# Fewer operations per reciprocal-root iteration, and VectorE in GpSimd's place for one group of subtractions

## The chip, the cores and the metric

The kernel runs on one core of a Trainium2 chip. The metric is the device time in microseconds (us) of one execution. The engines are called as the profile calls them: PE is TensorE (matmuls; PEld are its weight loads), DVE is VectorE, ACT is ScalarE, POOL is GpSimd, SP is SyncE, which here only issues DMAs. Each engine works through its own queue of instructions in order, and waits on semaphores for the others.

## The reference, cut to what matters

One layer of an encoder: a modulated RMSNorm of x (2048 tokens of width 1024), one wide input projection, two branches (neighbourhood attention with 8 heads, and a bidirectional mLSTM with 4 heads, run over chunks of tokens), an output projection, a residual sum and a last RMSNorm.

```python
h = rmsnorm(h_res, norm_w[l]) * (1.0 + scale[:, None, :]) + shift[:, None, :]
...
proj = h @ w_in + b_in
...
na_out = neighbourhood_attention(na_q, na_k, na_v, rpb) * jax.nn.silu(na_z)
...
hm = (h_fwd + h_bwd).transpose(0, 2, 1, 3) * jax.nn.sigmoid(ml_o).reshape(B, T, ML_HEADS, ML_HEAD_DIM)
mu = jnp.mean(hm, axis=-1, keepdims=True)
var = jnp.mean(jnp.square(hm - mu), axis=-1, keepdims=True)
hm = ((hm - mu) * lax.rsqrt(var + EPS)).reshape(B, T, ML_W) * ml_norm_w
...
return rmsnorm(h_res, final_norm_w).astype(x.dtype)
```

Reciprocal roots occur in three places: in the first RMSNorm, in the normalisation of `hm`, and in the last RMSNorm.

## The kernel before, in words

Every large product is computed in three passes over split operands: a float32 value is written as a high part (rounded to the matmul's format) and a low part (the rest), and the products high·high, high·low and low·high are summed. So each block of weights has to be split before PE can use it: ACT copies the raw weights into the high tile (`whi`), and another engine subtracts the high tile from the raw one to give the low tile (`wlo`).

The program has these stages. `start` (to about 142 us) loads x, computes the first norm's roots for four groups of four token tiles, transposes, and multiplies the first two weight blocks. `tok_blocks` and `conv_blocks` (to about 500 us) multiply further blocks and convolve. `phase1b` (to about 990 us) is the mLSTM: for each head a first pass (state updates `wv`, `dc`, `st`) and a second pass (scores `a`, weighted into `ck`; the sums `pi` and `px`, combined in `num`; the ratio `r`; the head output `hm`, its moments, its root `rstd`, its mean `mu`; then ACT normalises `hm`, and PE turns it into `ht`). The mLSTM's own matmuls are small, so PE is filled up with the rest of the input projection: `nq_gen` is a generator that yields after each of its matmuls (tile `pq`), and `pump(n)` draws n of them into the program between the mLSTM's steps. `phase2` is the attention and the output projection.

The projection inside `nq_gen` uses weight tiles of 128 columns, the *side weights*. Each is loaded by SP (`rawq`, L919) into the one buffer there is for it, split by `nq_split` into one half of `whi_a` and `wlo_a`, and used for one, two or four groups of 512 tokens. There are 30 such splits. In 20 of them (`s < 12`) the high part is a plain copy on ACT (L927) and POOL subtracts (L928). In the other 10, which hold the queries, ACT also scales (L930), and DVE makes the low part in one fused instruction (L931). The load of the next raw weights waits until the subtraction has read the buffer.

`rsqrt` (L1269) makes a reciprocal root on DVE: a first guess by integer operations on the bits (L1275, L1276), and three Newton iterations y ← y·(1.5 − 0.5·v·y²). With more than one value per partition an iteration has four instructions (L1282 to L1285); with one value the first two are fused (L1280). It is called four times in `start` (L251, four values per partition), 16 times in the mLSTM (L1210, four values) and 16 times in `phase2` (L1529, one value).

`start` and `phase2` are in an order written by hand. Between them a scheduler places each engine's instructions from the program's order and its own estimates, so a change of engine or of the number of operations there also moves neighbours.

Of the kernel before, what the change touches and what calls it, by code (L numbers as in the profile page):

```python
# [8 lines left out]
F32 = mybir.dt.float32  # L9
F32R = mybir.dt.float32r  # L10
AF = mybir.ActivationFunctionType
ALU = mybir.AluOpType
# [3 lines left out]
P = 128  # L16
# [42 lines left out]
class Kernel:  # L59
# [862 lines left out]
    def nq_split(self, i, s, raw):  # L922
        nc = self.nc
        hi, lo = self.wslot[0]
        cs = slice((i % 2) * P, (i % 2 + 1) * P)
        if s < 12:
            nc.scalar.activation(hi[:, :, cs], raw, AF.Copy)  # L927
            nc.gpsimd.tensor_tensor(lo[:, :, cs], raw, hi[:, :, cs].bitcast(F32), ALU.subtract)  # L928
        else:
            nc.scalar.activation(hi[:, :, cs], raw, AF.Copy, scale=-0.125)  # L930
            nc.vector.scalar_tensor_tensor(lo[:, :, cs], raw, -0.125, hi[:, :, cs].bitcast(F32), ALU.mult, ALU.subtract)  # L931
# [334 lines left out]
                    load_z(NG - 1)  # L1266
            yield

    def rsqrt(self, pool, y, v, nm, eng=None):  # L1269

        nc = self.nc
        eng = eng or nc.vector
        I32 = mybir.dt.int32
        n = y.shape[-1]
        nc.vector.tensor_scalar(y.bitcast(I32), v.bitcast(I32), 1, None, ALU.logical_shift_right)  # L1275
        nc.vector.tensor_scalar(y.bitcast(I32), y.bitcast(I32), -1, 0x5F3759DF, ALU.mult, ALU.add)  # L1276
        t = pool.tile([P, n], F32, tag="nwt", bufs=2, name=f"nwt_{nm}")
        for _ in range(3):
            if n == 1:
                nc.vector.scalar_tensor_tensor(t, y, v, y, ALU.mult, ALU.mult)  # L1280
            else:
                eng.tensor_tensor(t, y, y, ALU.mult)  # L1282
                eng.tensor_tensor(t, t, v, ALU.mult)
            eng.tensor_scalar(t, t, -0.5, 1.5, ALU.mult, ALU.add)
            eng.tensor_tensor(y, y, t, ALU.mult)  # L1285


    def phase2(self):
        nc = self.nc
# [427 lines left out]
```

## Time and profile before

| | |
|---|---|
| runs shown | 1376.62, 1380.95, 1381.31 us (median 1380.95) |
| profiled execution | 1379.22 us, its span 1377.2 us |
| granted PE clock, mean of the span | 0.988 |
| low parts of side weights on POOL (L928) | 20 instructions, 48.4 us |
| low parts of side weights on DVE (L931) | 10 instructions, 12.3 us |

The profile is of one execution. Its span runs from the first to the last instruction. A row of a group gives the line, the engine, the operation, written tile and read tiles, the count, then busy us and mean ns, then the idle time ahead of it with what ended it. A row of the timeline gives start and duration in us; in brackets stands how long the engine had been idle, and for whom it waited. A row of waits gives total us, times, and the longest. The granted clock is 1.00 or 0.50 at any moment, so a mean just under one means a few short slow windows.

### The profile page before, as it was taken

Reading aid. Unit: us, or ns where it says so; the run is one execution under the profiler, and the core shown is the slowest. Engines: PE = TensorE matmul, PEld = TensorE weight load, DVE = VectorE, ACT = ScalarE, POOL = GpSimd, SP = SyncE. Lnnn points to the kernel's source line nnn. Section 1 sums busy time; section 2 is a strip of 40 time slices with the busy share of each in tenths; the row PEclk is TensorE's granted clock in tenths of the full one; section 3 lists DMA queues with packets and bytes.
Section 4 is the critical chain, followed back from the end, with each engine's and each line's share of the span. In section 5 each row is a group of like instructions: output and inputs, shape, how many; then the busy total and the mean of one; then the engine's idle time right before and its main releaser. Section 6 shows DMA issues by size and latency. Waiting matters only on the chain. (4 is left out here: it accounts for less than half of the span.)

```text
span 1377.2 us, 23246 instructions
## 1 busy us (share of the span) xinstructions
PE 1303.8 (95%) x8026; PEld 1115.6 (81%) x8026; DVE 812.0 (59%) x2583; ACT 556.1 (40%) x1178; POOL 233.0 (17%) x266
## 2 busy tenths in 40 slices
PE   2999998999999999999999998999989999999996
PEld 2899998999877788888888787788766888888885
DVE  4744323111374696267768777877546777777774
ACT  5875445432231332113323233333336555555551
POOL 1000222433010110111121012121202111112111
PEclk9999999999999999999999999999989999999998
DMA  9996487766276876455757969746788897876862
GB/s 367 286 301 147 115 219 225 209 183 192 62 176 171 209 190 184 134 163 156 227 181 214 269 196 236 210 130 177 188 221 227 196 213 169 204 184 174 193 156 76
DMA packets 272010, 266.22 MB, mean 193 GB/s; under 512 B 32746, under 2 KB 234634, under 8 KB 271894
## 3 DMA queue, kind: packets, MB, share of 16 engines
q1 hardware_dynamic: 175870, 183.58, 48.8%
q0 software_dynamic: 21632, 38.40, 11.5%
q10 hardware_dynamic: 74392, 42.76, 10.8%
q8 instruction: 64, 1.05, 0.3%
q14 instruction: 52, 0.43, 0.1%
HBM read 179.14 MB, written 93.71 MB: 198 GB/s over the span
## 5 line engine op out<-in xcount | busy, mean ns | idle before, releaser
L954 PE MATMUL pq<-hhi,whi_a 128*128 128x512 f32 x512 | 212.2, 414 | 0.0
L954 PE MATMUL pq<-hlo,whi_a 128*128 128x512 f32 x512 | 212.0, 414 | 0.0
L954 PE MATMUL pq<-hhi,wlo_a 128*128 128x512 f32 x512 | 211.6, 413 | 0.0
L1435 ACT ACTIVATE pbuf<-pbuf,mn 128x480 f32<-128x480 f32 (+5 forms) x128 | 76.4, 597 | 122.3 <-DVE mn L1434 109.1
L954 PEld LDWEIGHTS pq<-hhi,whi_a 128*128 128x128 f32 x512 | 98.6, 193 | 18.4
L954 PEld LDWEIGHTS pq<-hhi,wlo_a 128*128 128x128 f32 x512 | 98.5, 192 | 18.4
L954 PEld LDWEIGHTS pq<-hlo,whi_a 128*128 128x128 f32 x512 | 98.6, 193 | 18.0
L1508 PE MATMUL y<-hhi,whi_a 128*128 128x512 f32 x256 | 84.8, 400 | 0.4 <-ACT whi_a L1481 0.4
L1508 PE MATMUL y<-hhi,wlo_a 128*128 128x512 f32 x256 | 84.4, 399 | 0.0
L1434 DVE CUSTOM_DVE_ANT_0 pbuf<-pS,tab 128x480 f32<-128x480 f32 (+5 forms) x128 | 64.9, 540 | 31.9 <-DMA tab<-d_t 15.9
L1180 ACT ACTIVATE num<-px,gtile 128x129 f32<-128x129 f32 x120 | 38.3, 365 | 98.4 <-PE px L1175 85.4
L928 POOL TENSOR_TENSOR wlo_a<-rawq,whi_a 128x1024 fp32r<-128x1024 f32 x20 | 48.4, 2421 | 163.1 <-ACT whi_a L927 122.1
L1107 DVE TENSOR_SCALAR wv<-kv,gtile 128x129 f32<-128x129 f32 x120 | 37.5, 318 | 61.4 <-PE dc L1123 33.4
L1199 POOL TENSOR_TENSOR hm<-hm,ck 128x128 f32<-128x128 f32 x64 | 26.5, 414 | 263.1 <-DVE hm L1198 220.5
L1471 PE MATMUL pO<-pt,v 128*64 128x128 f32 (+3 forms) x832 | 62.1, 283 | 8.7 <-ACT pt L1458 7.3
L803 ACT ACTIVATE dec<-dec,gtile 128x128 f32<-128x128 f32 x128 | 41.5, 391 | 66.8 <-POOL dec L799 54.4
L1471 PEld LDWEIGHTS pO<-pt,v 128*64 128x64 f32 (+3 forms) x832 | 45.8, 137 | 25.4 <-issue 12.9
L1456 PE MATMUL pT<-ident,pbuf 128*128 128x128 f32 (+2 forms) x416 | 59.9, 283 | 2.1 <-DVE pbuf L1446 2.1
L568 DVE TENSOR_TENSOR stv<-pv,brow 128x256 f32<-128x256 f32 x32 | 12.9, 423 | 78.9 <-PE pv L535 41.8
L1458 ACT ACTIVATE pt<-pT 96x384 f32<-96x384 f32 (+3 forms) x128 | 57.6, 499 | 0.7 <-PE pT L1456 0.7
L1508 PEld LDWEIGHTS y<-hhi,whi_a 128*128 128x128 f32 x256 | 47.2, 188 | 10.0 <-ACT whi_a L1481 0.6
L1456 PEld LDWEIGHTS pT<-ident,pbuf 128*128 128x128 f32 (+2 forms) x416 | 44.2, 137 | 13.4 <-issue 9.6
(301 smaller groups left out, 3556.2 us busy)
## 6 DMA issues: line engine op xcount, KB each, us to landing
ck<-d_ck SPq DMA_DIRECT2D x64, 384.5 KB
kv<-d_ck SPq DMA_DIRECT2D x120, 128.5 KB
rawq<-in_w_main_dram SPq DMA_DIRECT2D x30, 512.0 KB
raw<-in_w_main_dram SPq DMA_DIRECT2D x20, 512.0 KB
x<-in_x_dram SPq DMA_DIRECT2D x16, 512.0 KB
wmod<-in_w_mod_dram SPq DMA_DIRECT2D x16, 512.0 KB
dec<-d_mneg SPq DMA_DIRECT2D x32, 256.0 KB
d_ck<-dec ACTq DMA_DIRECT2D x32, 256.0 KB
```

The source lines that it names most:

```text
L803: nc.scalar.activation(t[:, d, o, :], t[:, d, o, :], AF.Exp, bias=self.cols["g"][:, d, h, c : c + 1])
L928: nc.gpsimd.tensor_tensor(lo[:, :, cs], raw, hi[:, :, cs].bitcast(F32), ALU.subtract)
L954: nc.tensor.matmul(patch_ps(ps) if patch else ps, w, self.htok(h, g, k, patch), start=(k == 0 and n == 0), stop=(k == KT - 1 and n == 2))
L1107: nc.vector.tensor_scalar(wv, tiles[d, i][:, 128:257], self.cols["w"][:, d, h, c : c + 1], None, ALU.mult)
L1180: nc.scalar.activation(num[:, d, :], px[:, d, :], AF.Copy, scale=self.cols["inter"][:, d, h, c : c + 1])
L1199: nc.gpsimd.tensor_tensor(t, t, vo.pop(c)[:, 129:257], ALU.mult)
L1434: nc.vector.tensor_tensor_reduce(pt[:, :nk], ps, tabs[place[u]][j][:, :nk], 1.0, 3e38, ALU.add, ALU.min, mn)
L1435: nc.scalar.activation(pt[:, :nk], pt[:, :nk], AF.Exp, bias=mn, scale=-1.0, accum_out=sums[:, j : j + 1])
L1456: nc.tensor.transpose(ps[:cs, i, :], pts[j][:, i * cs : (i + 1) * cs], self.ident)
L1458: nc.scalar.activation(t[:cs, :nch, :], ps[:cs, :nch, :], AF.Copy)
L1471: nc.tensor.matmul(po[j * HD : (j + 1) * HD, :], v[:n, h * HD : (h + 1) * HD], pt[j][:n, i, :], start=(i == 0), stop=(i == nch - 1))
L1508: nc.tensor.matmul(y, m[:, k, :], w[k][:, cs], start=(k == 4 and n == 0), stop=(k == 3 and n == 2))
```

## The change

In `nq_split` the subtraction of L928 is given to DVE; operands, shapes and result are the same. In `rsqrt` the constant −0.5 is taken out of the loop: w = −0.5·v is computed once per root into a new small tile (`nwv`), and an iteration is t = y², t = t·w, y = (t + 1.5)·y, the last two operations of that fused. A root of four values thus has 12 instructions instead of 14, and a root of one value 9 instead of 11. The argument `eng`, which no caller used, is gone. Behind `rsqrt` line numbers are one lower.

```diff
         if s < 12:
             nc.scalar.activation(hi[:, :, cs], raw, AF.Copy)
-            nc.gpsimd.tensor_tensor(lo[:, :, cs], raw, hi[:, :, cs].bitcast(F32), ALU.subtract)
+            nc.vector.tensor_tensor(lo[:, :, cs], raw, hi[:, :, cs].bitcast(F32), ALU.subtract)
...
+        w = pool.tile([P, n], F32, tag="nwv", bufs=2, name=f"nwv_{nm}")
+        nc.vector.tensor_scalar(w, v, -0.5, None, ALU.mult)
         t = pool.tile([P, n], F32, tag="nwt", bufs=2, name=f"nwt_{nm}")
         for _ in range(3):
             if n == 1:
-                nc.vector.scalar_tensor_tensor(t, y, v, y, ALU.mult, ALU.mult)
+                nc.vector.scalar_tensor_tensor(t, y, w, y, ALU.mult, ALU.mult)
             else:
-                eng.tensor_tensor(t, y, y, ALU.mult)
-                eng.tensor_tensor(t, t, v, ALU.mult)
-            eng.tensor_scalar(t, t, -0.5, 1.5, ALU.mult, ALU.add)
-            eng.tensor_tensor(y, y, t, ALU.mult)
+                nc.vector.tensor_tensor(t, y, y, ALU.mult)
+                nc.vector.tensor_tensor(t, t, w, ALU.mult)
+            nc.vector.scalar_tensor_tensor(y, t, 1.5, y, ALU.add, ALU.mult)
```

Three places show where the scheduler puts the moved subtraction; they are the places at 671, 836 and 873 us of the profile before, of which the prediction speaks. In the names the first number is the head (or the raw weight's turn), the next ones the step or chunk, the last one a running number of the tile.

DVE early in the first pass of head 1, where the last root of head 0 is finished (671 us), before:

```order
L1285 TENSOR_TENSOR rstd_0_3_6607<-rstd_0_3_6607,nwt_0_3_6611 128x4
L1133 SCALAR_TENSOR_TENSOR st_1_1_12_6690<-st_1_1_13_6666,gtile_1999,dc_1_2_6681 128x129
L1282 TENSOR_TENSOR nwt_0_3_6611<-rstd_0_3_6607 128x4
L1107 TENSOR_SCALAR wv_1_1_4_6686<-kv_1_1_11_6654,gtile_1999 128x129
L1283 TENSOR_TENSOR nwt_0_3_6611<-nwt_0_3_6611,var_0_3_6606 128x4
L1284 TENSOR_SCALAR nwt_0_3_6611<-nwt_0_3_6611 128x4
L1285 TENSOR_TENSOR rstd_0_3_6607<-rstd_0_3_6607,nwt_0_3_6611 128x4
L1212 SCALAR_TENSOR_TENSOR mu_0_3_6624<-mv_0_3_6434,rstd_0_3_6607 128x4
L1107 TENSOR_SCALAR wv_1_0_5_6713<-kv_1_0_5_6677,gtile_1999 128x129
```

The same place now:

```order
L1284 TENSOR_TENSOR nwt_0_3_6606<-nwt_0_3_6606,nwv_0_3_6604 128x4
L1133 SCALAR_TENSOR_TENSOR st_1_1_12_6682<-st_1_1_13_6658,gtile_1995,dc_1_2_6673 128x129
L1285 SCALAR_TENSOR_TENSOR rstd_0_3_6600<-nwt_0_3_6606,rstd_0_3_6600 128x4
L1107 TENSOR_SCALAR wv_1_1_4_6678<-kv_1_1_11_6646,gtile_1995 128x129
L1212 SCALAR_TENSOR_TENSOR mu_0_3_6616<-mv_0_3_6428,rstd_0_3_6600 128x4
L928 TENSOR_TENSOR wlo_a_123<-rawq_7_6498,whi_a_122 128x8x128
L1107 TENSOR_SCALAR wv_1_0_5_6705<-kv_1_0_5_6669,gtile_1995 128x129
```

The subtraction of the eighth raw weight stands on DVE behind `mu` and ahead of the `wv` of step 5; the root ends ahead of it.

DVE in the second pass of head 2 (836 us), before:

```order
L992 SCALAR_TENSOR_TENSOR qst_15_2_8565<-pq_15_2_8466,bcol_93,qst_15_2_8565 128x512
L1282 TENSOR_TENSOR nwt_2_1_8544<-rstd_2_1_8540 128x4
L1204 BN_STATS b6_2_8_8606<-hm_2_2_8531 128x6
L1283 TENSOR_TENSOR nwt_2_1_8544<-nwt_2_1_8544,var_2_1_8539 128x4
L1205 BN_AGGR mv_2_2_8532<-b6_2_8_8606 128x2
L1284 TENSOR_SCALAR nwt_2_1_8544<-nwt_2_1_8544 128x4
L1285 TENSOR_TENSOR rstd_2_1_8540<-rstd_2_1_8540,nwt_2_1_8544 128x4
L1212 SCALAR_TENSOR_TENSOR mu_2_1_8557<-mv_2_1_8326,rstd_2_1_8540 128x4
L1182 TENSOR_TENSOR num_2_9_8595<-num_2_9_8595,pi_2_9_8589 128x258
```

The same place now:

```order
L992 SCALAR_TENSOR_TENSOR qst_15_2_8551<-pq_15_2_8453,bcol_93,qst_15_2_8551 128x512
L1285 SCALAR_TENSOR_TENSOR rstd_2_1_8527<-nwt_2_1_8533,rstd_2_1_8527 128x4
L1204 BN_STATS b6_2_8_8592<-hm_2_2_8518 128x6
L1212 SCALAR_TENSOR_TENSOR mu_2_1_8543<-mv_2_1_8314,rstd_2_1_8527 128x4
L928 TENSOR_TENSOR wlo_a_123<-rawq_17_8390,whi_a_122 128x8x128
L1205 BN_AGGR mv_2_2_8519<-b6_2_8_8592 128x2
L1182 TENSOR_TENSOR num_2_9_8581<-num_2_9_8581,pi_2_9_8575 128x258
```

Here the subtraction stands behind `mu` too, but ahead of `num`, which PE's next `pi` needs.

DVE early in the first pass of head 3 (873 us), before:

```order
L1107 TENSOR_SCALAR wv_3_1_4_9010<-kv_3_1_11_8981,gtile_1999 128x129
L1282 TENSOR_TENSOR nwt_2_3_8933<-rstd_2_3_8929 128x4
L975 SCALAR_TENSOR_TENSOR hlo3_1231<-pq_9_0_8870,bcol_93,hlo3_1231 64x512
L1283 TENSOR_TENSOR nwt_2_3_8933<-nwt_2_3_8933,var_2_3_8928 128x4
L1133 SCALAR_TENSOR_TENSOR st_3_1_12_9014<-st_3_1_13_8994,gtile_1999,dc_3_2_9005 128x129
L1284 TENSOR_SCALAR nwt_2_3_8933<-nwt_2_3_8933 128x4
L1107 TENSOR_SCALAR wv_3_0_5_9038<-kv_3_0_5_9001,gtile_1999 128x129
```

The same place now:

```order
L1107 TENSOR_SCALAR wv_3_1_4_8994<-kv_3_1_11_8965,gtile_1995 128x129
L1285 SCALAR_TENSOR_TENSOR rstd_2_3_8914<-nwt_2_3_8920,rstd_2_3_8914 128x4
L975 SCALAR_TENSOR_TENSOR hlo3_1227<-pq_9_0_8855,bcol_93,hlo3_1227 64x512
L1212 SCALAR_TENSOR_TENSOR mu_2_3_8930<-mv_2_3_8738,rstd_2_3_8914 128x4
L1133 SCALAR_TENSOR_TENSOR st_3_1_12_8998<-st_3_1_13_8978,gtile_1995,dc_3_2_8989 128x129
L928 TENSOR_TENSOR wlo_a_123<-rawq_19_8785,whi_a_122 128x8x128
L1107 TENSOR_SCALAR wv_3_0_5_9022<-kv_3_0_5_8985,gtile_1995 128x129
```

Here it stands behind `wv_3_1_4` and two `st`, and ahead of the `wv` of step 5. On PE the order of the matmuls is as before but for three turns of `ht`, moved by a few places; on SP seven loads of raw weights come later, most of them by one or two loads of `kv` or `ck`.

More of the change, by code (lines that the diff above doesn't have):

```diff
@@ L1267, in ml_pass2, with rsqrt @@
             yield
-    def rsqrt(self, pool, y, v, nm, eng=None):
+    def rsqrt(self, pool, y, v, nm):
         nc = self.nc
-        eng = eng or nc.vector
         I32 = mybir.dt.int32
```

## The prediction

> **What bounds the kernel now.** I read the page first, then the list of what each engine waited for, then the timeline at the places where TensorE (PE) stood still.
>
> ```profile
> span 1377.2 us, 23246 instructions
> PE 1303.8 (95%) x8026; PEld 1115.6 (81%) x8026; DVE 812.0 (59%) x2583; ACT 556.1 (40%) x1178; POOL 233.0 (17%) x266
> ...
> PEclk9999999999999999999999999999989999999998
> ```
>
> PE works nearly all the time, in order, and its matmuls do not change here. The change can therefore move the time only through the moments in which PE waits, and through the clock that PE is granted. VectorE (DVE) at 59% and GpSimd (POOL) at 17% cost nothing as such. These are the largest of PE's waits over the run; columns are total us, times, longest.
>
> ```profile
> PE tp L264 <- ACT x L257: 21.7, 5, 19.6
> PE pO L1471 <- ACT pt L1458: 7.3, 2, 6.5
> ...
> PE dc L1123 <- DVE wv L1107: 4.9, 5, 2.1
> ...
> PE a L1162 <- DMA ck<-d_ck: 2.8, 3, 2.0
> ...
> PE ht L1232 <- ACT hm L1224: 1.9, 2, 1.5
> PE pi L1177 <- DVE num L1182: 1.6, 1, 1.6
> ```
>
> The first is the start, before any weight is multiplied, and a reciprocal root stands in it. The second belongs to the attention stage, which the change leaves alone but for its roots. The last four lie in the mLSTM stage, where the moved subtraction lives. What does POOL's subtraction (L928) cost there today? The first two rows are groups (mean ns after the comma), the others give the spread of the steps of a root (min/median/max ns).
>
> ```profile
> L928 POOL TENSOR_TENSOR wlo_a<-rawq,whi_a 128x1024 fp32r<-128x1024 f32 x20 | 48.4, 2421 | 163.1 <-ACT whi_a L927 122.1 <-PE dc L1123 30.5 <-PE pq L954 5.5
> L1410 DVE TENSOR_TENSOR hlo<-hlo,hhi 128x1024 fp32r<-128x1024 f32 x8 | 9.4, 1221 | 2.0 <-ACT hhi L1409 1.9
> ...
> L1284 DVE TENSOR_SCALAR nwt<-nwt x48: 136/164/2235, 618.2 to 973.2; 128x4 f32<-128x4 f32 x48
> L1285 DVE TENSOR_TENSOR rstd<-rstd,nwt x48: 145/163/2353, 618.5 to 973.4; 128x4 f32<-128x4 f32 x48
> ```
>
> A step of a root over four numbers per partition takes 0.16 us, yet sometimes more than 2 us. The timeline says when: each time POOL's subtraction has just begun. Below are three such moments, each with POOL's row, DVE's row and the PE wait that follows (start, duration, engine).
>
> ```profile
> 671.19 2.39 POOL L928 TENSOR_TENSOR wlo_a<-rawq,whi_a 128x1024 fp32r<-128x1024 f32 x1 [3.51 <-ACT whi_a L927]
> 671.24 2.35 DVE L1285 TENSOR_TENSOR rstd<-rstd,nwt 128x4 f32<-128x4 f32 x1
> 675.43 0.33 PE L1232 MATMUL ht<-perm,hm 128*128 128x128 f32 x1 [1.48 <-ACT hm L1224]
> ...
> 836.79 2.38 POOL L928 TENSOR_TENSOR wlo_a<-rawq,whi_a 128x1024 fp32r<-128x1024 f32 x1 [3.64 <-ACT whi_a L927]
> 836.95 2.23 DVE L1284 TENSOR_SCALAR nwt<-nwt 128x4 f32<-128x4 f32 x1
> 839.98 0.71 PE L1177 MATMUL pi<-ck 128*128 128x129 f32 x4 [1.56 <-DVE num L1182]
> ...
> 873.30 2.34 POOL L928 TENSOR_TENSOR wlo_a<-rawq,whi_a 128x1024 fp32r<-128x1024 f32 x1 [2.79 <-ACT whi_a L927]
> 873.64 2.03 DVE L1285 TENSOR_TENSOR rstd<-rstd,nwt 128x4 f32<-128x4 f32 x1
> 875.92 0.53 PE L1123 MATMUL dc<-wv,kv 128*128 128x129 f32 x2 [2.14 <-DVE wv L1107]
> ```
>
> In all three DVE's small instruction ends when POOL's ends (671.24+2.35 = 673.59 against 673.58; 839.18 against 839.17; 875.67 against 875.64), so DVE stood behind POOL and did not compute. After the third wait the clock also falls. Columns here: window, its length, then busy us of the engines with counts, and the granted clock.
>
> ```profile
> 848.90:852.30 3.40, 3.40 (x11) 2.75 (x11) 2.48 (x13) 0.00 (x0) 0.31 (x1) 0.50 1.03 186
> 876.20:879.60 3.40, 3.40 (x12) 2.68 (x11) 3.30 (x18) 0.38 (x1) 0.00 (x0) 0.50 0.85 243
> ...
> 880.00:883.40 3.40, 3.40 (x21) 2.91 (x21) 2.77 (x10) 1.56 (x4) 0.00 (x0) 1.00 0.56 153
> ```
>
> Twelve matmuls fit in 3.4 us at clock 0.50, twenty-one at 1.00: such a window loses half its length, 1.7 us.
>
> **The change, part by part.** *First root, at the start.* Fourteen DVE steps lie between these rows, and ACT's scaling of x, for which PE waits, starts after the last.
>
> ```profile
> 15.50 0.17 DVE L1275 TENSOR_SCALAR rst<-ssq 128x4 int32<-128x4 int32 x1
> ...
> 18.09 0.16 DVE L1285 TENSOR_TENSOR rst<-rst,nwt_x 128x4 f32<-128x4 f32 x1
> ...
> 18.29 2.19 ACT L257 ACTIVATE x<-x,rst 128x1024 f32<-128x1024 f32 x2 [3.03 <-DVE rst L1285]
> ```
>
> From the first start to the last is 2.59 us for thirteen steps, 0.20 each. Two steps fewer give −0.4 us; if the new fused step is as slow as the fused step of the last root below (0.25 instead of 0.20, three times), −0.25. I take −0.4. *Second root.* It ends in the same way for the next four tiles of x, and PE waits 0.44 us there:
>
> ```profile
> 57.15 0.33 PE L264 MATMUL tp<-ident,x 128*128 128x128 f32 x1 [0.44 <-ACT x L257]
> ```
>
> Two steps fewer take −0.4 of it; the bound on the other side is 0, if something else is late there. I take −0.4, the third and fourth roots at 0: PE works through other products while they run, and its wait for x above has no further long entry.
>
> *Roots of the mLSTM stage (16) and of the attention stage (all but the last of 16).* Two instructions of 0.16 us fewer in each, off the path while PE has fill products to work on. Taken at 0 apart from what the moments above include; if that cover were gone, 31 × 0.33 = 10 us is what they hold, no part of which shows as a PE wait on a root.
>
> *Last root.* Nothing follows it but two scalings and the output.
>
> ```profile
> 1366.95 1.26 POOL L1516 TENSOR_TENSOR xr<-xr,fnw 128x512 f32<-128x512 f32 x1 [0.43 <-ACT y L1514]
> ...
> 1367.67 0.56 DVE L1280 SCALAR_TENSOR_TENSOR nwt_f<-frs,fvar 128x1 f32<-128x1 f32 x1
> 1368.27 0.15 DVE L1284 TENSOR_SCALAR nwt_f<-nwt_f 128x1 f32<-128x1 f32 x1
> ...
> 1368.65 0.22 DVE L1280 SCALAR_TENSOR_TENSOR nwt_f<-frs,fvar 128x1 f32<-128x1 f32 x1
> ...
> 1369.72 0.16 DVE L1285 TENSOR_TENSOR frs<-frs,nwt_f 128x1 f32<-128x1 f32 x1
> ```
>
> The new multiplication by −0.5 (one step, 0.19) goes ahead of 1367.67 and is free: the first fused step waits until POOL's multiplication ends at 1368.21 anyway (0.56 instead of 0.22). After it, three pairs of steps (0.38 a pair) become three single fused steps of 0.19 to 0.25: −0.39 to −0.57. I take −0.45.
>
> *The moved subtraction.* POOL loses 20 × 2.42 us, DVE gains 20 × 1.22 (the row of L1410, same shape and operation). Gone is the standing behind POOL. What PE gets back at the three moments depends on where DVE's subtraction now stands; the program's order shows it. At 671 it comes after `mu`, for which PE waited there, so the whole 1.48 goes. At 836 it comes after `mu` but ahead of `num`: 1.22 takes the place of a stall of 2.23−0.16 = 2.07, and 1.56 becomes 0.7; −0.9. At 873 the `wv` for which PE waited now stands ahead of it, and the next `wv` is due one step of the loop later; 2.14 loses what the stall put in, 2.03−0.16 = 1.9. Sum −4.3, with bounds 0 (a new wait of the same size each time) and −5.4 (1.48+2.07+1.87, all that the stalls hold). The slow-clock window that follows the third wait goes with it, −1.7; bound 0.
>
> Now the cost of the new place. DVE is in order: behind the subtraction stand `num`, `wv`, `ck`, for which PE waits, and ahead of it the high part from ACT must be ready. The nearest rows are the ten splits that DVE does already (L931):
>
> ```profile
> L931 DVE SCALAR_TENSOR_TENSOR wlo_a<-rawq,whi_a 128x1024 fp32r<-128x1024 f32 x10 | 12.3, 1226 | 6.4 <-ACT whi_a L930 3.9 <-DMA d_qna<-qst 1.5 <-PE pq L954 0.8
> ...
> PE ht L1232 <- ACT hm L1224: 0.4, 1, 0.4
> ```
>
> They wait 0.64 us each. The second row is all that PE waited from 953 to 990 us, where four of them lie. I count that 0.4 against the eight that run before 990: 0.05 each, +1.0 for twenty. The upper bound comes from today's stalls: three of twenty subtractions reached PE, which at 1.22+0.64 each time would be 5.6; I double it, since every one now stands in DVE's queue: +11. The row of L931 is the same instruction in the same code, so I stay near it.
>
> *Queues.* One more engine waits for the subtraction: the next load of raw weights, and all behind it on SP's queue.
>
> ```profile
> SPq L919 <- POOL wlo_a L928: 54.7, 18, 8.4
> ```
>
> At half the duration it is released about 1.2 us sooner where DVE reaches the subtraction at once, and about as now where DVE comes 1.2 us late: 0. A few loads of raw weights change places with one load of `kv` or `ck`; rawq is loaded a whole turn ahead: 0.
>
> The Trainium skill's page "SBUF — State Buffer", section "Who interferes with whom", has a rule for what the three moments show: a VectorE instruction with two SBUF inputs and a GpSimd instruction that reads SBUF contend, and the later one blocks until the first ends. By that rule the trace agrees at the stall of `rstd` (two SBUF inputs, 2.35 us). The same rule speaks against the change: the subtraction on DVE has two SBUF inputs too and would now hold POOL's `hm` multiplication; what that would come to, worked out from rows, is the third rival.
>
> **Sum.** −0.4 −0.4 −4.3 −1.7 +1.0 −0.45 = −6.25. The profiled execution took 1379.22 us (span 1377.2 and 2.0 around it): 1373.0. The median shown, 1380.95, is 1.7 above it, the lowest run 2.6 below it.
>
> **The rivals.** *One stall for another.* DVE is held at the same moments, 1.22 us and a wait for ACT in place of 2; the waits move but stay, and only the roots count: 1379.22 − 1.25 = 1378. For it: 1.22+0.64 is nearly the 2.07 of today. Against: the order at 671 and 873. Chance 0.33.
>
> *More than the three.* At 846 PE waits again, and a slow window follows (848.90, above):
>
> ```profile
> 848.66 0.58 PE L1162 MATMUL a<-ck 128*128 128x128 f32 x2 [2.01 <-DMA ck<-d_ck]
> ```
>
> The `ck` load waits for POOL's `hm`, that for DVE, which worked without a pause since the stall at 836. If that goes too, −2.0 −1.7: 1369.3. Against: PE itself comes earlier there, so the gap may stay. Chance 0.17.
>
> *Slower: DVE holds POOL and itself.* The subtraction waits for ACT in DVE's queue, then holds POOL's `hm`, so `ck` loads and `num` come late. A row that bears on it: POOL's subtraction at 504.42 took 0.55 longer than its mean, begun within a two-input instruction of DVE.
>
> ```profile
> 504.36 0.74 DVE L897 SCALAR_TENSOR_TENSOR acc_q<-u,cw,acc_q 128x512 f32<-128x512 f32 x1
> 504.42 2.95 POOL L928 TENSOR_TENSOR wlo_a<-rawq,whi_a 128x1024 fp32r<-128x1024 f32 x1 [6.05 <-ACT whi_a L927]
> ```
>
> At +11 and three slow windows more (+5), with the roots' −1.25: 1394; it decides from 0.4 us of PE wait per subtraction on (20 × 0.4 = 8 over the 7.25 gained by the rest). Chance 0.07, for the bulk of it between 1386 and 1394.
>
> *The forecast* has 0.43, its own range 1369.5 to 1376.5.
>
> **Numbers.** Half a per cent, 6.9 us, is about what a measurement can tell from no change; faster by that is below 1374.0. Faster takes the second rival and 0.27 of the forecast's 0.43: 0.44. Slower is the third: 0.07. The rest, 0.49, is within. The range runs from 1366 (another 3 us below the second rival for waits for `kv`) to 1381 (the first rival and 3 us of new waits).
>
> **What would show it.** In the mLSTM stage no step of a root takes more than 0.3 us; L928 is on DVE at 1.22 with some 0.6 us idle ahead of it; PE's waits for `wv`, `num` and `hm` sum to under half of today's 8.4; one slow window fewer between 840 and 890; `frs` ends 0.4 sooner before the end. Wrong would be: PE waits of one to two us behind L928 on DVE, POOL's `hm` above 0.42 us or late, new windows of clock 0.50.

## The result, and the profile after

The changed kernel takes 1373.08 us, the kernel before 1381.09 us (medians of 20 runs each); the ratio of the runs is 0.9942, 95% interval 0.9927 to 0.9958. One of the 20 runs of the changed kernel took 1603.43 us at a mean granted clock of 0.752, and the ratio leaves it out. In a second measurement, with its own runs of the kernel before (run `after_again` below), the ratio is 0.9956 (0.9935 to 0.9978). So the change gains 8.0 us by the first and 6.1 by the second, and by their intervals between 3 and 10. The forecast of 1373.0 was met; that it was met to 0.1 us is luck, since 6.25 us were taken off an execution of 1379.22, and the medians are 8.0 apart. Its reasons were met only in part.

The profiled execution took 1377.13 us, 4 us above the median: it is one of the longer executions. The page:

```profile
span 1375.4 us, 23168 instructions
PE 1304.4 (95%) x8026; PEld 1117.3 (81%) x8026; DVE 797.4 (58%) x2531; ACT 556.7 (40%) x1178; POOL 186.8 (14%) x246
...
PEclk9999999999999999999999999999989999999998
```

PE does the same work in the same time (1303.8 us before). POOL is 46 us less busy. DVE took on 24.4 us of subtractions and lost 72 small steps of some 0.16 us (11 us), and yet it is 15 us less busy than before: what remains, some 28 us, is for the most part time that it stood still inside its instructions. The groups of the subtraction and of the steps of the mLSTM's roots show that (the first is a group with its idle time, the others give min/median/max in ns):

```profile
L928 DVE TENSOR_TENSOR wlo_a<-rawq,whi_a 128x1024 fp32r<-128x1024 f32 x20 | 24.4, 1220 | 12.2 <-ACT whi_a L927 11.1 <-PE pi L1177 1.0
...
L1284 DVE TENSOR_TENSOR nwt<-nwt,nwv x48: 146/157/338, 617.3 to 974.1; 128x4 f32<-128x4 f32 x48
L1285 DVE SCALAR_TENSOR_TENSOR rstd<-nwt,rstd x48: 129/156/336, 617.5 to 974.3; 128x4 f32<-128x4 f32 x48
```

The longest of these steps falls from 2.35 us to 0.34. Call an instruction of DVE *held* when it lasts over 0.15 us longer than the median of its group. Between 545 and 985 us the trace of before has 21 held instructions with 21.7 us of excess, that of after 5 with 1.1 us; over the whole span the excess falls from 35.8 to 10.6 us.

PE's waits, on the other hand, did not shrink as forecast (total us, times, longest):

```profile
PE dc L1123 <- DVE wv L1107: 4.8, 6, 1.6
...
PE px L1175 <- ACT num L1180: 3.7, 2, 2.6
PE ht L1232 <- ACT hm L1224: 3.6, 3, 2.5
...
PE a L1162 <- DMA ck<-d_ck: 2.9, 1, 2.9
```

At the third of the three moments the root now runs through without a pause, and PE waits all the same, one step later:

```profile
877.07 0.15 DVE L1285 SCALAR_TENSOR_TENSOR rstd<-nwt,rstd 128x4 f32<-128x4 f32 x1
...
878.59 0.76 DVE L975 SCALAR_TENSOR_TENSOR hlo<-pq,bcol,hlo 64x512 fp32r<-64x512 f32 x1 [1.36 <-ACT hlo L974]
879.37 0.16 DVE L1212 SCALAR_TENSOR_TENSOR mu<-mv,rstd 128x4 f32<-128x4 f32 x1
...
880.18 0.33 PE L1232 MATMUL ht<-perm,hm 128*128 128x128 f32 x1 [2.51 <-ACT hm L1224]
```

PE comes through `dc` without the stop that it had before and reaches `ht` before `mu` is there: between the root's last step (877.07) and `mu` DVE's queue holds L975, the low part of a side product, which waits 1.36 us for its high part from ACT.

The slow-clock windows at 848.9 and 876.2 us are gone, and others stand elsewhere. Columns as in the forecast: window, length, busy us with counts, and the granted clock behind POOL's column.

```profile
410.90:414.30 3.40, 3.40 (x10) 2.62 (x9) 3.34 (x7) 0.00 (x0) 1.07 (x1) 0.50 0.54 181
776.10:779.50 3.40, 3.40 (x13) 2.79 (x12) 3.39 (x13) 0.00 (x0) 0.00 (x0) 0.50 0.89 268
848.90:852.30 3.40, 2.85 (x18) 2.54 (x19) 2.62 (x15) 0.19 (x1) 0.41 (x1) 1.00 1.05 204
```

So one pair of profiles cannot say where 8 us went. The runs below gave twelve more, and their stretches can be averaged.

### The profile page after: what moved, and what is told of

Its sections match the earlier page's. It is cut to its first block, busy times and chain, and to the rows that moved or that the text cites. A ratio compares the mean times of both kernels' runs of the same rounds, so it can differ in the third digit from the quotient of the medians.

```text
span 1375.4 us, 23168 instructions
## 1 busy us (share of the span) xinstructions
PE 1304.4 (95%) x8026; PEld 1117.3 (81%) x8026; DVE 797.4 (58%) x2531; ACT 556.7 (40%) x1178; POOL 186.8 (14%) x246
## 5 line engine op out<-in xcount | busy, mean ns | idle before, releaser
L1107 DVE TENSOR_SCALAR wv<-kv,gtile 128x129 f32<-128x129 f32 x120 | 32.5, 284 | 54.1 <-PE dc L1123 27.4
L1507 PEld LDWEIGHTS y<-hhi,wlo_a 128*128 128x128 f32 x256 | 47.5, 188 | 9.3
```

The source lines that it names most:

```text
L1107: nc.vector.tensor_scalar(wv, tiles[d, i][:, 128:257], self.cols["w"][:, d, h, c : c + 1], None, ALU.mult)
L1507: nc.tensor.matmul(y, m[:, k, :], w[k][:, cs], start=(k == 4 and n == 0), stop=(k == 3 and n == 2))
```

## The experiments

All ratios are to the kernel before on the same chip, from 5 to 12 runs of each kernel and 17 to 29 of the kernel before, with a 95% interval. `after` stands for the changed kernel.

| run | what differs | ratio (interval) | held, 545–985 us | steps of a root, or `mu` behind it, held over 1 us |
|---|---|---|---|---|
| lo_only | before, subtraction on DVE | 0.9962 (0.9945–0.9979) | 6, 1.5 us | 0 |
| roots_only | before, new roots | 0.9965 (0.9946–0.9985) | 18, 14.6 us | 3 |
| pool_pieces | before, subtraction on POOL in 4 pieces | 1.0011 (0.9994–1.0029) | 40, 15.1 us | 0 |
| dve_twice | after, subtraction done twice | 0.9929 (0.9905–0.9952) | 6, 1.3 us | 0 |
| roots_start | before, new roots in `start` only | 0.9985 (0.9967–1.0002) | 21, 21.2 us | 6 |
| roots_ml | before, new roots in the mLSTM only | 0.9959 (0.9939–0.9979) | 18, 14.8 us | 3 |
| pool_twice | before, POOL's subtraction done twice | 1.0138 (1.0115–1.0162) | 37, 49.0 us | 11 |
| none_dve | after, one eighth of the subtraction | 0.9959 (0.9941–0.9978) | 3, 0.9 us | 0 |
| after_again | the changed kernel | 0.9956 (0.9935–0.9978) | 4, 1.1 us | 0 |
| pool_behind | after, a POOL operation of that shape behind the subtraction | 0.9931 (0.9909–0.9954) | 19, 14.0 us | 0 |
| all_dve | after, L200 on DVE too | 1.0035 (1.0015–1.0055) | 5, 1.0 us | 0 |
| pool_later | before, the split issued two k-steps later | 1.0001 (0.9979–1.0023) | 21, 22.4 us | 7 |

The kernel before has 21 held instructions with 21.7 us; in the last column it has 7.

### The two halves alone

```diff
 lo_only (before, with)
-            nc.gpsimd.tensor_tensor(lo[:, :, cs], raw, hi[:, :, cs].bitcast(F32), ALU.subtract)
+            nc.vector.tensor_tensor(lo[:, :, cs], raw, hi[:, :, cs].bitcast(F32), ALU.subtract)
 roots_only (before, with the new rsqrt; L928 stays on GpSimd)
```

> The subtraction on VectorE, the roots as before. Theory 1 (the gain is the standing of VectorE behind GpSimd's subtraction): 4 to 6 us below the kernel before, no step of a root above 0.4 us in the mLSTM stage. Theory 2 (the gain is the shorter roots, at the start, at the end and in the mLSTM chain): within 1.5 us of the kernel before. Theory 3 (one stall for another): 0, with PE waits behind the subtraction on VectorE that are as long in sum as before.

> The shorter roots, the subtraction left on GpSimd. Theory 1: 1.3 to 2 us below the kernel before (0.4 at the start, up to 0.7 more by the last group of x, 0.45 at the end), steps of roots still up to 2.4 us beside the subtraction. Theory 2: 5 to 8 us below, the whole of the change. Theory 3: as theory 1, and it is all that the change brings.

Measured: 0.9962 and 0.9965. Against 1376.4 us, the median of before there, that is −5.2 us (−2.9 to −7.6) for the move and −4.8 us (−2.1 to −7.4) for the roots. The move does what theory 1 expected; for the roots 4.8 lies between theories 1 and 2, and the forecast's 1.25 us lie outside the interval. Alone they sum to 10.0, together they gave 8.0 and 6.1; within the intervals that could still be a plain sum. A reason for an overlap is seen at the subtraction near 633 us in `roots_ml` (below), where the shorter root ends before POOL begins:

```profile
633.08 0.13 DVE L1304 SCALAR_TENSOR_TENSOR rstd<-nwt,rstd 128x4 f32<-128x4 f32 x1
633.25 0.16 DVE L1212 SCALAR_TENSOR_TENSOR mu<-mv,rstd 128x4 f32<-128x4 f32 x1
633.63 2.41 POOL L928 TENSOR_TENSOR wlo_a<-rawq,whi_a 128x1024 fp32r<-128x1024 f32 x1 [1.01 <-PE px L1175]
```

At the same place of the kernel before the root's last step is caught for 2.35 us:

```profile
639.46 2.38 POOL L928 TENSOR_TENSOR wlo_a<-rawq,whi_a 128x1024 fp32r<-128x1024 f32 x1 [0.97 <-PE px L1175]
639.51 2.35 DVE L1285 TENSOR_TENSOR rstd<-rstd,nwt 128x4 f32<-128x4 f32 x1
```

### Which roots

```diff
 roots_start: only the four calls in start
-            self.rsqrt(xp, rst[g], ssq[g], f"x{g}")
+            self.rsqrt_new(xp, rst[g], ssq[g], f"x{g}")
 roots_ml: only the calls in the mLSTM
-                self.rsqrt(ml, y, v, f"{h}_{gi}")
+                self.rsqrt_new(ml, y, v, f"{h}_{gi}")
```

> The kernel before with the shorter root only in the four roots of the first norm; the order of everything else is as before. Theory A (what the roots bring beyond my 1.25 us lies at the start: PE reaches every later stage earlier): 3 to 5 us below the kernel before. Theory B (it lies in the mLSTM stage, where a shorter root meets GpSimd's subtraction less often): 0.8 to 1.2 us below, as in my sum.

> The kernel before with the shorter root only in the 16 roots of the mLSTM stage. Theory A: within 1 us of the kernel before. Theory B: 3 to 4 us below, with fewer steps held by GpSimd's subtraction (the sum of what VectorE is held between 545 and 985 us falls from 21.7 to some 15 us, as in the run with all the roots).

Measured: 0.9985 (−2.1 us, between −4.5 and +0.3) and 0.9959 (−5.6 us, between −2.9 and −8.4). By these two values most of what the roots give comes from the mLSTM, where the forecast had put nothing, as theory B said; but the two intervals overlap. The profile of `roots_ml` has its held root steps down from 7 to 3, though its mLSTM stage, in that one execution, is not shorter (466.8 us from the first `pq` to the first `pS`, where the kernel before has 460.6).

### What the subtraction costs on either engine

```diff
 pool_pieces (before)
+            for k in range(0, KT, 2):
+                nc.gpsimd.tensor_tensor(lo[:, k : k + 2, cs], raw[:, k : k + 2], hi[:, k : k + 2, cs].bitcast(F32), ALU.subtract)
 pool_twice (before): the line of L928 stands twice
 dve_twice (after): the line of L928 stands twice
 none_dve (after)
+            nc.vector.tensor_tensor(lo[:, 0:1, cs], raw[:, 0:1], hi[:, 0:1, cs].bitcast(F32), ALU.subtract)
```

In `none_dve` seven eighths of the low parts of these weights are left out.

> The kernel before, with GpSimd's subtraction cut into four pieces of a quarter each, so that VectorE can stand behind at most one piece (some 0.65 us) at a time if it gets in between. Theory 1: 2 to 5 us below the kernel before, steps of roots up to 0.7 us and none above 1. Theories 2 and 3: no change, within 1.5 us.

> The kernel before with GpSimd making each of the 20 subtractions twice, so that VectorE can be held twice as long. If being held behind GpSimd is what costs (my theory): the held time doubles to some 40 us, and the kernel is 4 to 8 us slower than before. If the gain of the move came from the scheduler's other order of its neighbours or from chance: within 1.5 us of the kernel before.

> The changed kernel with VectorE making each of the 20 subtractions twice, the same result written again: 20 x 1.22 us more on VectorE. My sum takes 0.05 us of PE wait for each subtraction there: 1 to 2 us above the changed kernel, 4 to 6 below the kernel before. Theory 3 (the place on VectorE costs PE as much as the stall did): 4 to 6 us above the changed kernel, so level with the kernel before or slower.

> The changed kernel with only an eighth of each of the 20 subtractions (the first of 8 slices; the other low parts are left out), so neither engine holds the other long. It bounds what the subtraction still costs on VectorE: by my sum 1 us below the changed kernel (7 below the kernel before); if its place on VectorE costs PE as much as a stall did, 4 to 6 us below the changed kernel.

On DVE the subtraction is free as far as can be measured: twice of it gives 0.9929, an eighth of it 0.9959, the change itself 0.9942 and 0.9956. By the intervals the twenty cost at most 1 to 4 us, according to which two of these ratios are compared; the forecast's upper bound of 11 us is excluded.

On POOL a second one costs 1.38%, 19 us, far more than expected. It is almost all in the mLSTM stage (482.8 us from the first `pq` to the first `pS`, where the other kernels with the subtraction on POOL have 464.6 in the mean), and the trace of `pool_twice` shows how the two add up:

```profile
848.45 2.35 POOL L928 TENSOR_TENSOR wlo_a<-rawq,whi_a 128x1024 fp32r<-128x1024 f32 x1 [5.92 <-ACT whi_a L927]
848.62 2.20 DVE L1285 TENSOR_SCALAR nwt<-nwt 128x4 f32<-128x4 f32 x1
850.85 0.16 DVE L1286 TENSOR_TENSOR rstd<-rstd,nwt 128x4 f32<-128x4 f32 x1
850.87 2.35 POOL L929 TENSOR_TENSOR wlo_a<-rawq,whi_a 128x1024 fp32r<-128x1024 f32 x1
851.05 2.19 DVE L1213 SCALAR_TENSOR_TENSOR mu<-mv,rstd 128x4 f32<-128x4 f32 x1
853.63 0.58 PE L1178 MATMUL pi<-ck 128*128 128x129 f32 x1 [3.58 <-DVE num L1183]
```

DVE gets one instruction through between the two and is caught again, and PE waits 3.58 us for `num` behind it. In this stage PE's waits are for `wv`, `hm`, `num`, `st` and the loads of `ck`; none is for the low parts.

Four pieces (1.0011) bring nothing, against the 2 to 5 us of theory 1. DVE is held at piece after piece, 40 times instead of 21, for 15.1 us in all, and POOL needs 58.1 us for the eighty pieces instead of 48.4. Which of the two undoes the gain is not shown.

### Is it being held, as such?

```diff
 pool_behind (after): GpSimd adds the low parts to themselves, behind DVE's subtraction
             nc.vector.tensor_tensor(lo[:, :, cs], raw, hi[:, :, cs].bitcast(F32), ALU.subtract)
+            nc.gpsimd.tensor_tensor(lo[:, :, cs], lo[:, :, cs].bitcast(F32), lo[:, :, cs].bitcast(F32), ALU.add)
 pool_later (before): the split of the next side weights goes two k-steps further back
-                    if k == 2 and n == 0:
+                    if k == (4 if raw[1] < 12 else 2) and n == 0:
                         if needs and needs[0] == i + 1:
```

> The changed kernel once more, as the yardstick for the two runs beside it, and as a second profile of the same program. Both theories: the ratio of the first measurement, 0.9942 (0.9927 to 0.9958). In its mLSTM stage no step of a root should be held for more than 0.3 us, as in the first profile. If the waits of PE that were new in the first profile (px 2.56 us at 859.8, ht 2.51 us at 877.7, ck 2.91 us at 846.5) belong to the program, they stand here too, within 0.3 us of their length; if they move with the moment at which the clock falls or a load lands, other ones stand here and the sum of PE's gaps from 545 to 985 us, 16.0 there, differs by several us.

> The changed kernel with one GpSimd instruction of the old shape put behind VectorE's subtraction: it adds the low parts to themselves in place, so the low parts of these weights come out doubled. The raw weights are free again as early as in the changed kernel; only VectorE stands behind GpSimd again, and the low parts are ready some 2.4 us later. Theory C (the loss is VectorE being held by GpSimd's instruction): the gain of the moved subtraction goes, 5 us or more, and the ratio to before is that of the roots alone, 0.9965, or higher; root steps of over 2 us are back and VectorE's held time in the mLSTM stage is 10 to 25 us. Theory D (the loss came from the raw weights' buffer, released later by GpSimd, and the loads behind it on SP's queue): it stays at the changed kernel's time, 0.994, within 2 us.

> The kernel before, with its four-step roots and with GpSimd's subtraction, which is only issued two k-steps (six fill matmuls, at least 1.4 us) later in each turn, together with the copy of the high part and the next load of raw weights. Nothing is shorter here. Theory R (what cost time was GpSimd's subtraction falling on the steps of a root, which PE's next ht and num hang on; in the kernel before seven root steps of 2.0 to 2.4 us, in the run with GpSimd's addition behind VectorE's subtraction none, though VectorE was held for 14 us there too): the roots end before the subtraction begins, at most three root steps are held for over 1 us, and the time falls by 3 to 5 us, ratio 0.9965 to 0.998. Theory C (any held time of VectorE costs): VectorE is held as long as before, some 20 us, in num, r and wv, and the ratio is 1.000. Theory S (what the roots gave was their own length, 32 steps of 0.16 us in the mLSTM stage): 1.000 too, whatever is held. If other root steps are hit as often as now, the run tells nothing between R and C.

`after_again` repeats the first measurement within its interval, without long held root steps. Of the three waits of PE that were new in the profile of after, two stand there again within 0.1 us (`ht` 2.45, `ck` 2.96), and the third is shorter (`px`, 1.75 for 2.56).

`pool_behind` brought the holding back and not the loss: 0.9931, beside 0.9956 for the changed kernel on the same chip. POOL is busy with 38.7 us of it, and two of its twenty places show what it does:

```profile
L929 POOL TENSOR_TENSOR wlo_a<-wlo_a 128x1024 fp32r<-128x1024 f32 x20 | 38.7, 1933 | 177.5 <-DVE wlo_a L928 119.3 <-DVE u L864 34.1 <-PE dc L1124 9.3
...
684.20 2.14 DVE L1108 TENSOR_SCALAR wv<-kv,gtile 128x129 f32<-128x129 f32 x2
684.36 1.89 POOL L929 TENSOR_TENSOR wlo_a<-wlo_a 128x1024 fp32r<-128x1024 f32 x1 [14.14 <-DVE wlo_a L928]
...
832.83 1.89 POOL L929 TENSOR_TENSOR wlo_a<-wlo_a 128x1024 fp32r<-128x1024 f32 x1 [6.13 <-DVE mv L1206]
833.12 1.62 DVE L1190 SCALAR_TENSOR_TENSOR r<-num,gtile 128x2 f32<-128x2 f32 x1
```

DVE is held for 14.0 us there, all but 1.0 of it in `r` and `wv`, in no long step of a root. So theory C, that any held time of DVE costs, falls, and what theory D expected is what came: the changed kernel's time or a little less. Three readings are left. One, R, is that it matters which instruction is held: the kernels with six or more in the last column have 0.9985 and above, those with three or none 0.9965 and below, but for `all_dve`, which loses in another stage (below), and `pool_pieces`, where steps of the roots and `mu` are held fourteen times for 0.3 to 0.55 us. The second, D, is that the raw weights' buffer is released sooner. SP did wait less ahead of the next load of raw weights in after: 74.9 us in all, whatever it waited for, where before has 110.8. The forecast has 54.7 us for this row:

```profile
SPq L919 <- DVE wlo_a L928: 21.4, 10, 6.8
```

Against D stands that `roots_ml` gains as much with POOL's late release, and that PE's waits for `ck`, which stands behind that load in SP's queue, are no shorter after (2.9 us, 2.8 before). The third is that the scheduler's new order of the neighbours helps by itself: all kernels with the subtraction on DVE have such an order, and none of them has long held root steps, so no run parts this reading from R.

`pool_later` was to part R from the rest by moving POOL's subtraction off the roots, and did not move it. At the place of 836 us, for one, the copy on ACT, which it waits for, kept its place in ACT's queue behind the same copy of a product (L991), and the subtraction began where it began before (836.79).

```profile
834.85 0.69 ACT L991 ACTIVATE qst<-pq,bcol 128x512 fp32r<-128x512 f32 x1 [3.81 <-PE px L1175]
835.44 1.05 ACT L927 ACTIVATE whi_a<-rawq 128x1024 fp32r<-128x1024 f32 x1
...
836.57 2.39 POOL L928 TENSOR_TENSOR wlo_a<-rawq,whi_a 128x1024 fp32r<-128x1024 f32 x1 [2.49 <-ACT whi_a L927]
836.73 2.25 DVE L1284 TENSOR_SCALAR nwt<-nwt 128x4 f32<-128x4 f32 x1
```

Seven root steps are held as before, and the ratio is 1.0001: the run tells nothing between R and C. Nor does it test the expectation's theory S, that the shorter roots help by their own length. That the held roots are the cause thus stays likely and not shown.

### A version meant to beat both

```diff
 all_dve (after), in load_w
-            nc.gpsimd.tensor_tensor(lo[:, ks, :256], raw, hi[:, ks, :256].bitcast(F32), ALU.subtract)
+            nc.vector.tensor_tensor(lo[:, ks, :256], raw, hi[:, ks, :256].bitcast(F32), ALU.subtract)
```

> The changed kernel with GpSimd's other subtractions of low parts also on VectorE, the 14 half blocks of the token and convolution weights (L200; 2.4 to 2.6 us each on GpSimd). VectorE is held there for 9.1 us in 5 instructions by the changed kernel's profile (129 to 545 us). Theory C, at the rate that the moved subtraction showed (20 us less held time for 5.2 us): 2 us faster than the changed kernel, ratio to before about 0.9925. Rival (PE has matmuls to work on through all of these, its gaps from 129 to 545 us are 9.6 us and hang on other things): no difference, 0.994. Third: VectorE's epilogues come later behind 14 x 1.22 us more work and PE waits for its accumulators: 2 to 5 us slower than the changed kernel, 0.996 to 0.998.

Measured: 1.0035, 10.9 us slower than the changed kernel beside it (0.9956): the third case, at over twice its price. The trace shows one place that is worth half of it. There DVE stands still for 14.81 us, with the low part of a weight block at the head of its queue and the high part not yet copied, and PE waits behind it for `stvo` to clear an accumulator:

```profile
247.21 1.99 ACT L199 ACTIVATE whi_b<-raw 128x1024 fp32r<-128x1024 f32 x2
248.28 1.22 DVE L200 TENSOR_TENSOR wlo_b<-raw,whi_b 128x1024 fp32r<-128x1024 f32 x1 [14.81 <-ACT whi_b L199]
...
249.42 0.42 DVE L588 TENSOR_TENSOR stvo<-pvo,brow 128x256 f32<-128x256 f32 x1
...
249.89 0.58 PE L533 MATMUL pv<-whi_a,hhi 128*128 128x256 f32 x1 [5.50 <-DVE stvo L588]
```

With L200 on POOL, PE has no wait of over 0.3 us between 225 and 260 us (traces of after and `after_again`). The same move that helps at L928, where DVE waits 0.61 us for ACT, hurts at L200.

### The stretches of fourteen profiles

Each kernel left one profile. Mean durations from row to row of their traces, in us, with the number of profiles in brackets and ± the standard error:

| stretch, and what it is parted by | old | new | difference |
|---|---|---|---|
| start to the first `tp`; roots of `start` | 19.2 (6) | 18.5 (7) | −0.7 |
| start to the first `pv`; roots of `start` | 241.2 ± 0.6 (6) | 238.3 ± 0.3 (7) | −2.9 |
| first `pq` to first `pS`; subtraction on POOL or DVE | 464.6 ± 1.4 (6) | 459.4 ± 0.8 (7) | −5.2 |
| last `y` to the last step of `frs`; last root | 4.95 (7) | 4.37 (7) | −0.58 |

`all_dve` is left out of the first two rows and `pool_twice` of the third. Rows two to four sum to −8.7, beside −8.0 and −6.1 measured, and the third repeats what `lo_only` gave in time (−5.2). Of its DVE kernels all but `lo_only` (457.5) have the new roots too, of its POOL kernels two, and these two are not shorter than the other four (465.7 and 464.0): so the −5.6 of `roots_ml`, though measured, is not found in its stage, and how much of the mLSTM's gain the roots would give alone stays open. In that stage PE's waits of over 0.8 us sum to 12.8 us in the mean of the six with POOL and to 9.8 in the seven with DVE (difference −3.0, standard error 1.4). Its time at clock 0.50 is 6.8 us with POOL and 4.4 with DVE in the mean, 0 to 13.7 us in one profile; at half lost that is −1.2. Together they make 4.2 of the 5.2. Taken off each profile's stage, these waits and half of the time at clock 0.50 leave 446 to 450 us in all fourteen, `pool_twice` too (482.8 − 26.5 − 8.5 = 447.8). So the differences of the stage are PE's long waits and its slow windows, within 2 us or so; which held instructions make the waits is the open part. The kernel before has 9.0 us of such waits, the least of its six: the forecast was read from an execution with few waits.

## Why the prediction was right, point by point

- **The sum, −6.25 us: right in size, in part by luck.** Measured −8.0 and −6.1 us. For the move alone the forecast has −4.3 −1.7 +1.0 = −5.0, and −5.2 was measured, though not at the places that it names. For the roots it has −1.25, and −4.8 was measured alone; that both together gave 8.0 and 6.1 and not 10.0 is what keeps the forecast near.
- **First root, −0.4: right, a little small.** From the first integer step to the start of the last step the trace of after takes 1.98 us, where before took 2.59:

```profile
15.62 0.17 DVE L1274 TENSOR_SCALAR rst<-ssq 128x4 int32<-128x4 int32 x1
15.82 0.17 DVE L1275 TENSOR_SCALAR rst<-rst 128x4 int32<-128x4 int32 x1
15.90 0.16 DVE L1277 TENSOR_SCALAR nwv_x<-ssq 128x4 f32<-128x4 f32 x1
...
17.60 0.16 DVE L1285 SCALAR_TENSOR_TENSOR rst<-nwt_x,rst 128x4 f32<-128x4 f32 x1
```

  The multiplication by −0.5 (15.90) starts 0.08 us behind its neighbour and takes no place of its own, so three steps of 0.20 are saved and not two: −0.61. The fused step is as short as the others.
- **Second to fourth root, −0.4: too small, or something else was won.** Up to the first `pv` the mean gain is −2.9, and `roots_start` measured −2.1 in all (−4.5 to +0.3). How the 0.7 won at `tp` grows by then was not traced.
- **Last root, −0.45: right.** −0.58 from the last `y` on, in every kernel with the new root.
- **The roots of the mLSTM, 0: this term failed.** They were "Taken at 0 apart from what the moments above include"; with them alone the time fell by 5.6 us (2.9 to 8.4). One reason may be that a shorter root is hit less often, 3 times instead of 7; another is the length of their 32 steps of 0.16 us, and the runs do not part the two. Together with the rest they add less, as said above.
- **Three moments, −4.3: the size holds for the move, the places do not.** The moved subtraction alone gives −5.2. But the waits at the three places stay, smaller or at another step. The first two in after:

```profile
673.92 0.33 PE L1232 MATMUL ht<-perm,hm 128*128 128x128 f32 x1 [0.77 <-ACT hm L1224]
...
839.08 0.60 PE L1175 MATMUL px<-st,ck 128*128 128x129 f32 x3 [1.15 <-ACT num L1180]
```

  In `after_again` they are 0.97 and 1.48. The third, 2.14 for `wv`, became 2.51 and 2.45 for `ht`, behind L975, and such a wait for `ht` (2.3 to 3.1 us) stands there in all seven kernels with the subtraction on DVE. In the mean of the profiles of the table's third row the waits of over 0.4 us at the three places go from 1.3, 1.3 and 2.7 us to 0.5, 0.7 and 2.6: −1.5 and not −4.3. That is the first rival, one stall for another, wholly at the third place and in part at the others. The criterion "under half of today's 8.4" failed: `wv`, `num` and `hm` sum to 12.1 in after (10.1 in `after_again`). The forecast priced three waits of one execution; the gain is in the sum over the stage, in other waits and in slow windows. Its bound of −5.4 also counts the whole stall of 2.07 at 836, where PE waited 1.56.
- **One slow window, −1.7: not shown.** The two windows near 850 and 876 are gone, but two of the same length stand at 410.9 and 776.1, which are not there before. A slow window begins between 871 and 881 us in five of the seven profiles with POOL and in four of the seven with DVE, where no step of a root is held for over 1 us; so it does not hang on the held root alone.
- **More than the three (the rival): did not come.** The wait for `ck`, 2.01 us before, is 2.91 in after and 2.96 in `after_again`.
- **DVE's new place, +1.0: too much, but within what can be measured.** The idle time ahead of L928 is 12.2/20 = 0.61 us, as forecast (0.64); no cost is seen when it is doubled.
- **Slower, DVE holds POOL: the mechanism is there, the price is not.** (The 2.95 us of the forecast's row are 0.53 above the mean of 2.42, not 0.55.) Twice in after POOL's `hm` multiplication starts inside DVE's subtraction and is held:

```profile
703.58 1.22 DVE L928 TENSOR_TENSOR wlo_a<-rawq,whi_a 128x1024 fp32r<-128x1024 f32 x1
703.74 1.33 POOL L1199 TENSOR_TENSOR hm<-hm,ck 128x128 f32<-128x128 f32 x1 [3.71 <-DVE hm L1198]
```

  It takes 1.33 us (1.25 the other time, at 940.50) instead of 0.41, and no wait of PE over 0.8 us follows within 30 us. The Trainium skill's page "SBUF — State Buffer", section "Who interferes with whom", says that whichever of the two is issued first makes the other wait; the trace agrees in this direction too (1.33 us) as in the other (2.35 us).

## What to carry to other kernels

Judge an operation on GpSimd not by its length alone but also by the VectorE instructions that fall into it: a 0.16 us step that starts inside a 2.4 us subtraction of GpSimd lasts until the subtraction ends, and cutting the subtraction into pieces did not help. That it matters which instruction falls into it is likely from these runs, and not shown: 14.0 us of held `r` and `wv` cost nothing that could be measured. Moving it to VectorE pays where its input is ready when VectorE reaches it (0.6 us of waiting here) and costs where VectorE would stand at the head of its queue for it (14.8 us at L200). And a saving of half a per cent is not read from two profiles: take the stretch from several, since the waits of one execution are a sample.

## What was not expected of the hardware

A step with a single tensor input is held just as one with two: `nwt` with four numbers (2.23 us at 836.95 before) and `wv` with 129:

```profile
689.17 2.40 POOL L928 TENSOR_TENSOR wlo_a<-rawq,whi_a 128x1024 fp32r<-128x1024 f32 x1 [15.60 <-PE dc L1123]
689.57 2.08 DVE L1107 TENSOR_SCALAR wv<-kv,gtile 128x129 f32<-128x129 f32 x1 [0.82 <-DMA kv<-d_ck]
```

Of the three moments of the forecast, the one at 836 is such a step with one input.

Windows of granted clock 0.50 last 3.4 us or a multiple, but for the one that the end of the program cuts off. Some stand at other places in each profile, as at 848.9 us before and at 410.9 and 776.1 after; others come back, as one that begins between 991 and 1025 us does in all fourteen. A window of 3.4 us is worth up to 1.7, which is a good part of the few us by which executions of one kernel differ. The Trainium skill's page "TensorE: Matmul & The Clock Gate", in its part 1 on the clock gate, says that the window of some 3.4 us in which PE's activity is judged runs freely and does not start with the kernel; the length agrees (3.40 us).
